# A feed-forward block's input differences: adding two pieces of a stored matrix in PSUM by products with the identity, instead of subtracting them one after the other

## The chip, the cores and the metric

The kernel runs on one core of a Trainium2 chip. The metric is the device time of one execution in microseconds (us), taken as the median of several. Five engines of the core work from lists of their own, each strictly in its list's order: TensorE (PE in the profile, with PEld for its weight loads) multiplies matrices into PSUM, VectorE (DVE), ScalarE (ACT) and GpSimd (POOL) work element by element, and SyncE (SP) issues the DMAs. They wait for one another through semaphores.

## The reference, cut to what matters

One layer: a norm, a combined projection, three kinds of mixing (Fourier, attention, gated delta rule), an output projection, and a squared-ReLU feed-forward block over 1024 positions with 1024 channels and 4096 hidden channels. The change lies in the last step, where the normed input `h` of the feed-forward block is prepared and multiplied by `w_ff1`.

```python
def _mlp(h, w1, w2):
    u = jnp.maximum(h @ w1, 0.0)
    return (u * u) @ w2

def _layer(x, xc, c, c_ctx, rope, lp, ctx_out):
    ...
    x = x + g1 * _mix_out(P, o_att, o_dn, lp['w_out'], lp['o_norm'])
    x = x + g2 * _mlp(_rms(x, lp['norm2']) * (1 + sc2) + sh2, lp['w_ff1'], lp['w_ff2'])
    ...
```

## The kernel before, in words

**Two pieces for one number.** Matrix products are done in a rounded float32 format in which one multiplication pass is enough. To keep accuracy every operand is cut in two: `hi` is the operand rounded (a copy, on ACT unless said otherwise), `lo` is the operand minus `hi`. `split` (L1452 to L1454) does this: L1453 is the rounding, L1454 the subtraction on the engine that it is given. A product is then three matmuls, hi by hi, hi by lo and lo by hi (`mm3`, L238 to L241).

**Seven products in place of eight.** The product `h @ w1` is cut into 2 by 2 blocks and done with seven block products instead of eight, which needs sums and differences of blocks on both sides. On the side of `h` the blocks are "11" and "21" (channels 0 to 511 and 512 to 1023 of the first 512 positions) and "12" and "22" (the same of the last 512 positions). Each is stored transposed, as four tiles k = 0 to 3 of 128 channels by 512 positions, with a hi and a lo piece each. `h2_first` (L1456) makes "11" and "21". `h2_second` (L1539) makes what the other products need: t1 = "12" - "11", t2 = "22" - t1, t3 = t2 - "11", t4 = t2 - "21", and "22" itself. A table (L1470) says which product takes which: s1 takes t1, s2 takes t2, s4 takes "22", s3 takes t3, and the product named 22 takes t4. The names 11 and 12 are the two products that need only what `h2_first` made.

**How h2_second works through its tiles.** `h2_T` (L1446) makes one tile: four transposes on PE (L244 in the profile, since the helper `tp` records them) into one PSUM bank, and one ACT instruction (L223, the helper `act`) that scales, shifts and moves the bank into SBUF. The banks come from the ring `tr2` of three, `bk0`, `bk1` and `bk3`. In a first loop over k, t1 is made from such a tile by two subtractions (L1540), first of the hi piece of "11", then of its lo piece, since only the pieces are kept. The first of the two is on POOL for k > 0 and on DVE for k = 0, the second on DVE. A second loop makes "22" and t2 (one subtraction). A third makes t3 and t4, each by two subtractions, the first on POOL, the second on DVE; the lo piece of t3 is also made on POOL.

**The products.** `ff1(j, name)` (L1564) does one of the seven products for 128 hidden channels, j counting them: 4 tiles by 3 matmuls of 128 by 512 into one bank of the ring `f1r`, which is A3[0], A3[1], A3[2], `bk2`, `bk3`, `bk4`. What follows in `ff1` takes the bank out: ACT for 11 and s1, DVE for the others (L1591 for 12, L1598 for s2, L1602 for s4, L1605 for s3, L1613 for 22), and makes the squares and sums that are stored to DRAM as `u`. So `bk3` serves both rings, and the s1 product of j = 0, which falls on `bk3`, can only come when `h2_second` is through with it. `w1_prep` (L1482) prepares the weight side: sums on POOL (L1487), hi pieces on ACT and lo pieces on DVE (`z1c` in the profile). `load_w1` (L1475) brings the weights (L1478 on SP's queue). `gate_bc` (L1347) makes rows of a gate with a short matmul into `bk0` and a DVE addition (L1352).

**What sets the order.** The kernel is written as one program; a scheduler at build time places the instructions of each engine in a fixed list by its own estimate of their times, with priorities given to pieces of the code. `h2_second` has such a priority (L1618), and so its instructions lie among those of the products 11 and 12 and of `w1_prep`. On the chip each engine keeps to its list. In the profile `fbase`, `rbase`, `z1c` and `z2b` are the large SBUF areas: `rbase` and `z2b` hold the pieces on the side of `h`, `z1c` those of the weights, `fbase` the full float32 tiles. `ba` and `bk` are the PSUM banks.

Of the kernel before, what the change touches and what calls it, by code (L numbers as in the profile page):

```python
# [14 lines left out]
ALU = mybir.AluOpType  # L15
AX = mybir.AxisListType

P = 128
# [176 lines left out]
def body(tc, t, out):  # L195
# [3 lines left out]
    with ctx:  # L199
# [14 lines left out]
        V, G, T, Y, SC = nc.vector, nc.gpsimd, nc.tensor, nc.sync, nc.scalar  # L214
# [4 lines left out]
        def rbuf(*shape, a=None):  # L219
            return Buf(a or Ra, (P,) + shape)  # L220
# [4 lines left out]
        def f32(ap):  # L225
            return ap.bitcast(F32)
# [8 lines left out]
        def mm(o, l, r, start, stop):  # L235
            pe(T.matmul(o, l, r, start=start, stop=stop))  # L236
# [15 lines left out]
        C = {k: cstb[a >= 256]()[:, a % 256 if a < 256 else a - 256 : b if a < 256 else b - 256] for k, (a, b) in CST.items()}  # L252
# [157 lines left out]
        for k, _ in enumerate(mod_steps(0, slabs, bk[2])):  # L410
            b = trb.next()
# [222 lines left out]
        b = gb.next()  # L634
# [795 lines left out]
        rw = [[buf(4, 256) for _ in range(2)], None]  # L1430
        shr = Ring([buf(512) for _ in range(3)])
        tr2 = Ring([bk[0], bk[1]])

        def rms_ff(q):
            st = rsb[q]()
# [16 lines left out]
        def split(i, hi, lo, eng, heng=None):  # L1452
            (heng or act)(hi, i)  # L1453
            eng.tensor_tensor(lo, i, f32(hi), op=ALU.subtract)  # L1454
# [82 lines left out]
        ur = Ring(slot[14:16] + slot[0:8:2] + slot[1:8:2] + slot[8:14])  # L1537

        def h2_second():  # L1539
            sub = lambda e, o, i, x: e.tensor_tensor(o, i, x, op=ALU.subtract)  # L1540
            t1, tr_ = [x() for x in slot[8:12]], Ring([x() for x in slot[12:14]])
            for k in range(4):
                h2_T(k, t1[k])
                sub(G if k > 0 else V, t1[k], t1[k], f32(HB["11"][k][0]))
                sub(V, t1[k], t1[k], f32(HB["11"][k][1]))
                split(t1[k], *HB["t1"][k], V)
            for k in range(4):
                h22 = tr_.next()
                h2_T(k + 4, h22)
                sub(V, t1[k], h22, t1[k])  # L1550
                split(t1[k], *HB["t2"][k], V)
                split(h22, *HB["22"][k], V)
            for k in range(4):
                x3 = tr_.next()
                sub(G, x3, t1[k], f32(HB["11"][k][0]))
                sub(V, x3, x3, f32(HB["11"][k][1]))
                split(x3, *HB["t3"][k], G)
                sub(G, t1[k], t1[k], f32(HB["21"][k][0]))
                sub(V, t1[k], t1[k], f32(HB["21"][k][1]))
                split(t1[k], *HB["t4"][k], V)  # L1560

        f1r = Ring(A3 + bk[2:5])
# [221 lines left out]
```

## Time and profile before

| | us |
|---|---|
| median of 3 runs (lowest, highest) | 1477.43 (1477.26, 1480.0) |
| the profiled execution: its own time | 1475.22 |
| its span on the core | 1473.1 |
| PE busy in the span | 1391.9 |
| DVE busy | 1026.7 |
| ACT busy | 704.6 |
| POOL busy | 657.2 |
| from 832.4 to 889.0, the stage of `h2_second`: length | 56.6 |
| in it: PE, DVE, ACT, POOL busy | 45.81, 53.34, 32.55, 43.45 |

The profiled execution lies 2.21 us under the median. The time outside the span is 1475.22 - 1473.1 = 2.1 us. Starts of instructions are counted in us from the start of the span. The column PEclk of a window is the TensorE clock that was granted in it, as a share of full speed.

### The profile page before, as it was taken

How to read it: one execution, taken by the hardware profiler on the slowest of the kernel's cores; microseconds unless marked ns; L12 is line 12 of the kernel's file. 1: busy time of each engine (PE TensorE's matmuls, PEld its weight loads, DVE VectorE, ACT ScalarE, POOL GpSimd, SP SyncE). 2: the span in 40 equal slices, each digit the busy share in tenths (PEclk: the TensorE clock that was granted, in tenths of full speed). 3: DMA queues.
4: the chain of work that ended last, by engine and by line, in shares of the span. 5: the costliest groups of instructions: out<-in, count | busy, mean ns of one | idle time of the engine just before them, and what ended most of it. 6: DMA issues, size and time to landing. Idle time of an engine off the chain costs nothing.

```text
span 1473.1 us, 28890 instructions
## 1 busy us (share of the span) xinstructions
PE 1391.9 (94%) x11438; PEld 1118.6 (76%) x11438; DVE 1026.7 (70%) x1747; ACT 704.6 (48%) x1239; POOL 657.2 (45%) x698
## 2 busy tenths in 40 slices
PE   5899888989999999989899789999999999999998
PEld 1787866766777777768799667888888888888886
DVE  0876688775878777786733898755556677676884
ACT  1743312223777777776512645554555443443331
POOL 2764653632446466465433866444343100020782
PEclk8799999989999999999999889999999999999999
DMA  9414374552001010042222214544445898776641
GB/s 327 176 58 141 95 186 122 148 109 79 9 9 25 5 36 10 10 148 72 87 82 105 92 49 143 164 152 156 158 157 185 296 395 271 249 236 210 200 158 57
DMA packets 137302, 197.65 MB, mean 134 GB/s; under 512 B 45021, under 2 KB 80463, under 8 KB 136911
## 3 DMA queue, kind: packets, MB, share of 16 engines
q1 hardware_dynamic: 136464, 195.12, 41.2%
q8 instruction: 89, 1.46, 0.4%
q10 hardware_dynamic: 703, 0.69, 0.2%
q14 instruction: 46, 0.38, 0.1%
HBM read 149.84 MB, written 45.94 MB: 133 GB/s over the span
## 4 chain that ended last, share of the span: by engine, by line
PE 46%; DVE 5%; POOL 2%; issue 1%; DMA 1%; ACT 0%; DVEq 0%; POOLq 0%; ACTq 0%; SPq 0%
PE bk L240 8%; PE bk L241 8%; PE bk L239 8%; PE ba L239 7%; PE ba L240 7%; PE ba L241 7%; DVE fbase L1540 1%; PE bk L236 1%; DVE z1c L1454 1%; DVE z1b L1321 0%; DVE rbase L984 0%; DMA fbase<-la 0%; POOL rbase L1454 0%; PE ba L236 0%; POOL z2c L1714 0%
## 5 line engine op out<-in xcount | busy, mean ns | idle before, releaser
L223 ACT ACTIVATE rbase<-fbase 128x512 fp32r<-128x512 f32 (+3 forms) x255 | 171.9, 686 | 87.6 <-PE bk L240 55.3
L223 ACT ACTIVATE fbase<-bk 128x512 f32<-128x512 f32 (+3 forms) x224 | 124.9, 561 | 150.8 <-PE bk L236 93.8
L236 PE MATMUL bk<-rbase 128*128 128x256 f32 (+1 forms) x960 | 164.5, 307 | 2.1 <-DVE rbase L984 1.1
L236 PEld LDWEIGHTS bk<-rbase 128*128 128x128 f32 (+1 forms) x960 | 127.0, 173 | 30.4 <-DVE rbase L984 1.9
L236 PE MATMUL ba<-rbase 128*65 128x512 f32 (+4 forms) x576 | 137.7, 341 | 6.3 <-DVE rbase L984 4.6
L223 ACT ACTIVATE z1c<-fbase 128x512 fp32r<-128x512 f32 (+1 forms) x120 | 76.7, 654 | 135.3 <-DMA fbase<-w_ff 49.1
L223 ACT ACTIVATE fbase<-fbase 128x512 f32<-128x512 f32 (+4 forms) x148 | 95.8, 660 | 94.5 <-POOL fbase L1606 27.2
L1487 POOL TENSOR_TENSOR fbase<-fbase 128x512 f32<-128x512 f32 x64 | 89.2, 1395 | 110.7 <-DVE z1c L1454 101.5
L1688 POOL TENSOR_TENSOR z2c<-z2c,fbase 128x512 f32<-128x512 f32 x16 | 31.8, 2010 | 203.6 <-ACT z2c L223 128.6
L960 DVE TENSOR_REDUCE fbase<-ba 128x1 f32<-128x512 f32 (+1 forms) x192 | 106.4, 594 | 19.6 <-PE ba L236 18.2
L223 ACT ACTIVATE rbase<-z1d 128x1024 fp32r<-128x1024 f32 x61 | 63.1, 1055 | 101.2 <-PE bk L240 87.3
L1454 DVE TENSOR_TENSOR z1c<-fbase,z1c 128x512 fp32r<-128x512 f32 x112 | 96.3, 866 | 19.2 <-ACT z1c L223 15.8
L1454 DVE TENSOR_TENSOR rbase<-z1d,rbase 128x1024 fp32r<-128x1024 f32 x61 | 85.5, 1416 | 31.8 <-ACT rbase L223 31.7
L984 POOL TENSOR_TENSOR rbase<-fbase,rbase 128x512 fp32r<-128x512 f32 x56 | 72.1, 1288 | 67.2 <-ACT rbase L223 63.1
L239 PE MATMUL bk<-rbase 128*128 128x512 f32 x256 | 99.6, 389 | 0.0
L240 PE MATMUL bk<-rbase 128*128 128x512 f32 x256 | 99.6, 389 | 0.0
L241 PE MATMUL bk<-rbase 128*128 128x512 f32 x256 | 99.6, 389 | 0.0
L984 DVE TENSOR_TENSOR rbase<-fbase,rbase 128x512 fp32r<-128x512 f32 x104 | 81.0, 779 | 24.6 <-ACT rbase L223 23.9
L1454 DVE TENSOR_TENSOR rbase<-fbase,rbase 128x1024 fp32r<-128x1024 f32 (+1 forms) x63 | 79.7, 1285 | 22.6 <-ACT rbase L223 22.5
L236 PEld LDWEIGHTS ba<-rbase 128*65 128x65 f32 (+1 forms) x576 | 75.7, 154 | 23.9 <-DVE rbase L984 5.7
L240 PE MATMUL ba<-rbase 128*128 128x512 f32 x192 | 74.7, 389 | 0.0
L241 PE MATMUL ba<-rbase 128*128 128x512 f32 x192 | 74.7, 389 | 0.0
(346 smaller groups left out, 3842.6 us busy)
## 6 DMA issues: line engine op xcount, KB each, us to landing
fbase<-w_ff SPq DMA_DIRECT2D x70, 512.0 KB
u<-fbase SPq DMA_DIRECT2D x112, 256.0 KB
z1d<-w_ff SPq DMA_DIRECT2D x34, 512.0 KB
z1d<-u SPq DMA_DIRECT2D x33, 512.0 KB
fbase<-w_mod SPq DMA_DIRECT2D x32, 512.0 KB
fbase<-u SPq DMA_DIRECT2D x23, 512.0 KB
z2a<-w_mod SPq DMA_DIRECT2D x16, 512.0 KB
fbase<-w_in SPq DMA_DIRECT2D x16, 512.0 KB
```

The source lines that it names most:

```text
L223: return SC.activation(o, i, f, **k)
L236: pe(T.matmul(o, l, r, start=start, stop=stop))
L239: pe(T.matmul(o, lh, rh, start=start, stop=False))
L240: pe(T.matmul(o, lh, rl, start=False, stop=False))
L241: pe(T.matmul(o, ll, rh, start=False, stop=stop))
L960: V.tensor_reduce(st4[:, z : z + 1], b, AX.X, ALU.max)
L984: (G if k2 in GP and not any(a <= n < b for a, b in NGP) else V).tensor_tensor(hl[:, :, 1], p, f32(hl[:, :, 0]), op=ALU.subtract)
L1454: eng.tensor_tensor(lo, i, f32(hi), op=ALU.subtract)
L1487: G.tensor_tensor(w[nm], w[a], w[b], op=op)
L1540: sub = lambda e, o, i, x: e.tensor_tensor(o, i, x, op=ALU.subtract)
L1688: G.tensor_tensor(c, c, G2[cs_.start // 512], op=ALU.mult)
```

## The change

The two subtractions of a stored block become one. PE adds hi and lo of a tile in a PSUM bank by two matmuls with an identity matrix as the stationary operand (`joined`), and DVE subtracts the bank from the tile. The bank comes from the ring `tr2`, in which the transposes also take theirs. This happens 12 times: four for t1, four for t3 and four for t4. No instruction of `h2_second` is on POOL any more; the lo piece of t3 is made on DVE. The identity is rounded once into the format of the products, into 128 columns of a buffer of its own.

```diff
@@ -1430,6 +1430,8 @@
         tr2 = Ring([bk[0], bk[1]])
+        idb = rbuf(P)
+        V.tensor_copy(idb(), C["ident"])
@@ -1537,26 +1539,30 @@
         def h2_second():
-            sub = lambda e, o, i, x: e.tensor_tensor(o, i, x, op=ALU.subtract)
+            sub = lambda o, i, x: V.tensor_tensor(o, i, x, op=ALU.subtract)
             t1, tr_ = [x() for x in slot[8:12]], Ring([x() for x in slot[12:14]])
+
+            def joined(nm, k):
+                b = tr2.next()
+                for z in range(2):
+                    mm(b, idb(), HB[nm][k][z], z == 0, z == 1)
+                return b
+
             for k in range(4):
                 h2_T(k, t1[k])
-                sub(G if k > 0 else V, t1[k], t1[k], f32(HB["11"][k][0]))
-                sub(V, t1[k], t1[k], f32(HB["11"][k][1]))
+                sub(t1[k], t1[k], joined("11", k))
                 split(t1[k], *HB["t1"][k], V)
             for k in range(4):
                 h22 = tr_.next()
                 h2_T(k + 4, h22)
-                sub(V, t1[k], h22, t1[k])
+                sub(t1[k], h22, t1[k])
                 split(t1[k], *HB["t2"][k], V)
                 split(h22, *HB["22"][k], V)
             for k in range(4):
                 x3 = tr_.next()
-                sub(G, x3, t1[k], f32(HB["11"][k][0]))
-                sub(V, x3, x3, f32(HB["11"][k][1]))
-                split(x3, *HB["t3"][k], G)
-                sub(G, t1[k], t1[k], f32(HB["21"][k][0]))
-                sub(V, t1[k], t1[k], f32(HB["21"][k][1]))
+                sub(x3, t1[k], joined("11", k))
+                split(x3, *HB["t3"][k], V)
+                sub(t1[k], t1[k], joined("21", k))
                 split(t1[k], *HB["t4"][k], V)
```

The scheduler places the lists anew between about 820 us and 930 us; ahead of that and behind it the lists of the compute engines hold the same instructions in the same order, with one more DVE copy for the identity. Lines behind the change have moved in the new file: the subtraction is L1542 (before L1540), the lo piece L1456 (L1454), and L1597, L1604, L1608, L1611, L1619 are the DVE evacuations of 12, s2, s4, s3 and 22. In the lists below `bk_76`, `bk_77`, `bk_78`, `bk_79` and `bk_80` are `bk0` to `bk4`, and `ba_73` to `ba_75` are A3[0] to A3[2].

TensorE, the first loop and the start of the second. First the list before: transposes for k = 3 to 7 (k = 0 to 2 were placed earlier), and the product s1 of j = 1 (`bk_80`, reading t1 from `z2b`).

```order
L244 MATMUL bk_79<-fbase 128x128 x4
L244 MATMUL bk_76<-fbase 128x128 x4
L244 MATMUL bk_77<-fbase 128x128 x4
L244 MATMUL bk_79<-fbase 128x128 x4
L239 MATMUL bk_80<-z2b,z1c 128x512
L244 MATMUL bk_76<-fbase 128x128 x4
L240 MATMUL bk_80<-z2b,z1c 128x512
```

The same place in the changed kernel:

```order
L236 MATMUL bk_79<-rbase 128x512 x2
L244 MATMUL bk_76<-fbase 128x128 x4
L236 MATMUL bk_77<-rbase 128x512 x2
L244 MATMUL bk_79<-fbase 128x128 x4
L239 MATMUL bk_80<-z2b,z1c 128x512
L240 MATMUL bk_80<-z2b,z1c 128x512
L241 MATMUL bk_80<-z2b,z1c 128x512
L236 MATMUL bk_76<-rbase 128x512 x2
L239 MATMUL bk_80<-z2b,z1c 128x512
L244 MATMUL bk_77<-fbase 128x128 x4
L240 MATMUL bk_80<-z2b,z1c 128x512
L241 MATMUL bk_80<-z2b,z1c 128x512
```

Joins (L236 of 128x512) stand between the groups of transposes in the same three banks, so that a group of transposes now follows a join out of a bank that DVE has to empty; the join for k = 0 stands a little ahead of this piece.

VectorE, from the end of the second loop into the third. The list before:

```order
L1540 TENSOR_TENSOR fbase<-fbase 128x512 x2
L1454 TENSOR_TENSOR rbase<-fbase,rbase 128x512 x4
L1540 TENSOR_TENSOR fbase<-fbase,rbase 128x512 x2
L1352 TENSOR_TENSOR fbase<-bk_76,fbase 128x256
L1454 TENSOR_TENSOR z1c<-fbase,z1c 128x512
L1540 TENSOR_TENSOR fbase<-fbase,rbase 128x512
L1454 TENSOR_TENSOR z1c<-fbase,z1c 128x512
L1540 TENSOR_TENSOR fbase<-fbase,rbase 128x512
```

And in the changed kernel:

```order
L1542 TENSOR_TENSOR fbase<-fbase 128x512 x2
L1456 TENSOR_TENSOR rbase<-fbase,rbase 128x512 x2
L1542 TENSOR_TENSOR fbase<-fbase,bk_79 128x512
L1456 TENSOR_TENSOR rbase<-fbase,rbase 128x512 x2
L1542 TENSOR_TENSOR fbase<-fbase,bk_76 128x512
L1542 TENSOR_TENSOR fbase<-fbase,bk_77 128x512
L1456 TENSOR_TENSOR rbase<-fbase,rbase 128x512
L1456 TENSOR_TENSOR z2b<-fbase,z2b 128x512
```

The subtractions of the third loop now read a PSUM bank and stand among the last lo pieces of the second loop, where before they came in a block behind it.

TensorE, the end of the third loop in the changed kernel:

```order
L236 MATMUL bk_76<-rbase 128x512 x2
L236 MATMUL bk_77<-rbase 128x512 x2
L240 MATMUL bk_80<-rbase,z1c 128x512
L236 MATMUL bk_79<-rbase 128x512 x2
L239 MATMUL ba_74<-z2b,z1c 128x512
L240 MATMUL ba_74<-z2b,z1c 128x512
L241 MATMUL ba_74<-z2b,z1c 128x512
L239 MATMUL ba_74<-z2b,z1c 128x512
L240 MATMUL ba_74<-z2b,z1c 128x512
L241 MATMUL ba_74<-z2b,z1c 128x512
L236 MATMUL bk_76<-rbase 128x512 x2
L239 MATMUL bk_79<-z2b,z1c 128x512
```

The last row is the start of the s1 product of j = 0 in `bk_79`. Before, that product came as soon as the last transposes had left the bank, in the middle of s2 and s4; now it follows the last joins, behind s2 and s4.

## The prediction

> **What bounds the kernel now.** I read the busy shares first, then the waits of PE, then windows around the stage of the change.
>
> ```profile
> span 1473.1 us, 28890 instructions
> PE 1391.9 (94%) x11438; PEld 1118.6 (76%) x11438; DVE 1026.7 (70%) x1747; ACT 704.6 (48%) x1239; POOL 657.2 (45%) x698
> ```
>
> PE is the bound over all, and the page alone would advise against giving it more work. The windows say where it is not. The first six columns are the window, its length, and the busy times of PE, PEld, DVE, ACT and POOL; then the granted clock.
>
> ```profile
> 834.30:849.00 14.70, 6.42 (x24) 3.99 (x23) 14.56 (x13) 10.75 (x19) 12.17 (x8) 0.60 0.30 90
> 849.00:855.00 6.00, 5.05 (x14) 3.48 (x13) 6.00 (x11) 5.31 (x10) 0.00 (x0) 0.57 0.12 45
> 855.00:870.00 15.00, 15.00 (x63) 11.21 (x62) 13.81 (x14) 5.77 (x10) 12.61 (x7) 1.00 0.02 3
> 870.00:880.00 10.00, 8.50 (x30) 5.31 (x29) 10.00 (x12) 4.11 (x7) 8.39 (x6) 0.90 0.33 101
> 880.00:885.00 5.00, 5.00 (x13) 3.39 (x11) 5.00 (x6) 2.12 (x5) 5.00 (x3) 0.51 0.02 3
> 893.20:1000.00 106.80, 106.05 (x459) 85.52 (x458) 76.24 (x107) 57.98 (x101) 50.12 (x36) 1.00 0.53 175
> 1000.00:1100.00 100.00, 100.00 (x434) 80.90 (x433) 56.30 (x86) 51.90 (x89) 42.84 (x31) 1.00 0.46 151
> ```
>
> From 834.3 to 885 DVE is busy without a break while PE idles or runs at half clock. Behind 893.2 PE has no idle time worth naming at full clock, so what PE gains before 893.2 reaches the end, and what it loses too. PE's longest wait in the stage, with total, count and longest, names who is late:
>
> ```profile
> PE bk L240 <- DVE z2b L1454: 5.8, 2, 4.9
> ```
>
> It is product s1 waiting for the lo pieces of t1. DVE's own work shows why, with POOL's beside it (count, busy, mean ns):
>
> ```profile
> L1540 DVE TENSOR_TENSOR fbase<-fbase,rbase 128x512 f32<-128x512 f32 x13 | 21.2, 1646 | 1.2 <-POOL fbase L1540 1.2
> L1454 DVE TENSOR_TENSOR z1c<-fbase,z1c 128x512 fp32r<-128x512 f32 x12 | 15.2, 1271 | 1.2 <-ACT z1c L223 1.2
> L1454 DVE TENSOR_TENSOR rbase<-fbase,rbase 128x512 fp32r<-128x512 f32 x8 | 5.1, 686 | 0.0
> L1591 DVE TENSOR_TENSOR fbase<-ba,fbase 128x512 f32<-128x512 f32 x1 | 0.7, 678 | 0.0
> L1540 POOL TENSOR_TENSOR fbase<-fbase,rbase 128x512 f32<-128x512 f32 x11 | 19.6, 1794 | 9.9 <-DVE rbase L1454 9.9
> L1454 POOL TENSOR_TENSOR z2b<-fbase,z2b 128x512 fp32r<-128x512 f32 x2 | 3.5, 1732 | 0.0
> L1454 POOL TENSOR_TENSOR rbase<-fbase,rbase 128x512 fp32r<-128x512 f32 x2 | 3.4, 1728 | 0.0
> ```
>
> The same kind of DVE instruction takes 686 ns or 1646: the long ones run beside POOL. L1591, which reads one operand from PSUM, takes 678, and not because POOL was quiet:
>
> ```profile
> 835.60 3.27 POOL L1487 TENSOR_TENSOR fbase<-fbase 128x512 f32<-128x512 f32 x2 [0.69 <-DVE z1c L1454]
> 835.98 0.68 DVE L1591 TENSOR_TENSOR fbase<-ba,fbase 128x512 f32<-128x512 f32 x1
> ```
>
> So a subtraction that reads a bank should keep its price beside POOL.
>
> **The unit prices.** From the timelines of PE and DVE:
>
> ```profile
> 816.61 0.60 PE L244 MATMUL bk<-fbase 128*128 128x128 f32 x4
> 816.97 0.37 PE L241 MATMUL ba<-z1c,rbase 128*128 128x256 f32 x1
> 848.45 0.80 PE L240 MATMUL bk<-z2b,z1c 128*128 128x512 f32 x1 [4.86 <-DVE z2b L1454]
> 851.05 0.80 PE L240 MATMUL bk<-z2b,z1c 128*128 128x512 f32 x1 [0.95 <-DVE z2b L1454]
> 854.66 0.39 PE L240 MATMUL ba<-rbase,z1c 128*128 128x512 f32 x1
> 854.89 0.40 PE L241 MATMUL ba<-rbase,z1c 128*128 128x512 f32 x1
> 879.49 0.79 PE L239 MATMUL ba<-rbase,z1c 128*128 128x512 f32 x1 [0.56 <-DVE fbase L1602]
> 883.50 0.63 PE L239 MATMUL ba<-rbase,z1c 128*128 128x512 f32 x1
> 883.93 0.63 PE L240 MATMUL ba<-rbase,z1c 128*128 128x512 f32 x1
> 884.91 0.69 PE L236 MATMUL bk<-fbase 1*128 1x256 f32 x2
> 885.53 0.74 PE L239 MATMUL ba<-z2b,z1c 128*128 128x512 f32 x2
> 893.22 0.39 PE L241 MATMUL bk<-rbase,z1c 128*128 128x512 f32 x1
> 849.11 0.69 DVE L1454 TENSOR_TENSOR z1c<-fbase,z1c 128x512 fp32r<-128x512 f32 x1
> 849.71 0.68 DVE L1540 TENSOR_TENSOR fbase<-fbase,rbase 128x512 f32<-128x512 f32 x1
> ```
>
> By their starts: a 128x512 matmul 0.233 us at full clock (854.66 to 854.89) and 0.43 at half; a group of four transposes 0.36; a gate row 0.62; a DVE instruction that is not held up 0.60. A join has the form of a product's matmul, so two cost 0.47.
>
> **The change part by part.** Removed: 13 DVE subtractions (21.2 us) and all of POOL's 11 (19.6), with POOL's four lo pieces of t3 (3.5 + 3.4). Added on DVE: 12 subtractions that read PSUM and 4 lo pieces, 16 at 0.60 = 9.6. Added on PE: 24 matmuls, 24 x 0.233 = 5.6 at full clock, 24 x 0.43 = 10.3 at half. The copy of the identity, one DVE instruction long before, is nothing: PE is the bound there. DVE's list from the first lo piece at 833.6 to the end of `h2_second` has 51 instructions now, 51 x 0.60 = 30.6, so it could be through by 864.2, where it now needs until
>
> ```profile
> 887.99 1.01 DVE L1454 TENSOR_TENSOR z1c<-fbase,z2b 128x512 fp32r<-128x512 f32 x1 [0.70 <-ACT z2b L223]
> ```
>
> It will not be, since it waits: for POOL's weight sums at first, for ACT's hi pieces in the second loop, for PE in the third. So I make the sum on PE, from 834.3, where its first long stall begins, to the last matmul of product 12 of j = 2, which starts at 893.22 and is the first point that both lists reach with the same products done.
>
> *Before:* 58.9 us elapsed for 144 matmuls x 0.233 = 33.6, five groups of transposes 1.8, four gate rows 2.5: 37.9 of work, 21.0 lost.
>
> *After:* 144 products and 22 joins (two come earlier), 166 x 0.233 = 38.7; six groups of transposes 2.2; three gate rows 1.9: 42.8 of work. Its losses, by walking the new lists with the prices above:
>
> - 834.3 to 849.5, the first loop. Nothing moves until ACT takes the first transposes out of their bank:
>
> ```profile
> 835.47 0.76 ACT L223 ACTIVATE fbase<-bk,fbase 128x512 f32<-128x512 f32 x1
> 833.63 2.43 DVE L1454 TENSOR_TENSOR z1c<-fbase,z1c 128x512 fp32r<-128x512 f32 x2 [1.23 <-ACT z1c L223]
> 837.66 3.43 DVE L1540 TENSOR_TENSOR fbase<-fbase,rbase 128x512 f32<-128x512 f32 x2
> ```
>
>  Then join 1 can go (836.3), and join and transposes alternate through three banks, each waiting for DVE or ACT, at half clock and without long gaps. DVE comes to the first subtraction at 837.7 as before, since the same weight pieces stand ahead of it (from 833.63), and is through with it at 838.3 in place of 841.1 (837.66 + 3.43, both pieces). The hi piece follows on ACT behind three others (0.5 to 0.7 each) by 839.6, the lo piece on DVE behind a second subtraction and one weight piece beside POOL by about 841, where the list before has it at 848.4 (the end of the 4.86 us wait); the last at 848.4. PE gets through six transpose groups, 8 joins and 14 products: 2.2 + 22 x 0.233 = 7.3 of 15.2 us. Lost 7.9.
> - 849.5 to 863.5: 48 products of s2 and s4 and 12 joins, 14.0, as the pieces come: two pairs are ready when it starts, the other two at about 855. Lost 0.
> - 863.5 to 870.6: product 22 of j = 1 needs the bank of s2, which DVE empties at 864.7 behind two lo pieces of weights; s1 of j = 0 needs the bank of the last t3 join (866.5). 22 products and a gate row take 5.7. Lost 1.4.
> - Behind that the last pieces, 0.4, and 1.3 as an estimate for the 0.1 us between engines at some dozen hand-overs that the walk passes over.
>
> Sum 7.9 + 1.4 + 0.4 + 1.3 = 11.0 lost, 53.8 elapsed: 888.1. One gate row that was in the sum before comes later now, 0.6. Gain 893.2 - 0.6 - 888.1 = 4.5 us. In the profiled execution 1475.2 becomes 1470.7; that lies 2.2 under the median, so **1477.4 - 4.5 = 1472.9, say 1473**. From both sides: with no loss at all the gain would be 893.2 - 0.6 - 834.3 - 42.8 = 15.5; with the old losses it would be 4.9 below nothing.
>
> What is late next: ACT, whose list holds weight pieces that wait for a DMA ahead of hi pieces of t3 and t4. The loads are issued when the old weights have been split:
>
> ```profile
> 868.59 3.87 SPq L1478 DMA_DIRECT2D fbase<-w_ff x2
> ACT z1c L223 <- DMA fbase<-w_ff: 3.4, 2, 2.5
> ```
>
> I let this cost nothing, because the hi pieces behind it are wanted only near 870; uncovered it is the 3.4 us of this row.
>
> **The clock, and a rule against the change.** At 851.05 PE starts a dense run at half clock, and at 854.66 it is at full: 3.6 us. The run from 879.49 needs some 6. Both are products without transposes between them. I let the joins, transposes and products from 838 on do the same by about 845. If only an unmixed run lifts the clock, it rises 3.6 us after 849.5, and half of the work of these 3.6 us is lost, 1.8: a gain of 2.7, 1474.7. That is a rival below. The Trainium skill, "TensorE: Matmul & The Clock Gate", Part 4 (PE-mode transpose), is the rule that speaks for it: transposes are not counted as activity. Its section on a second failure mode adds that cycling through PSUM banks can make the clock swing.
>
> **The rivals.** *DVE keeps its pace (slower).* Every join of the third loop waits for a bank that DVE empties, and the s1 product of j = 0, which helped to fill PE between 855 and 870, now stands behind them. So PE is tied to DVE's list. Behind DVE's last piece PE still has, by the new list, 62 matmuls and two gate rows, 15.7. If the 51 instructions take with their waits the mean of this stage,
>
> ```profile
> 832.40:889.00 56.60, 45.81 (x163) 31.95 (x164) 53.34 (x55) 32.55 (x55) 43.45 (x26) 0.79 0.15 47
> ```
>
> 53.34 / 55 = 0.97 us, the list ends at 883.1, and PE at 898.8 instead of 892.6: 6.2 slower, 1484. It decides from 0.85 us an instruction upward (892.6 - 15.7 - 833.6 = 43.3 over 51); my walk has 0.73. For it: POOL still has four weight sums from 835.60 on, and weight pieces beside such sums took 1271 ns in the mean. Against it: at 3.27 for two they end near 842, and 12 of 16 subtractions read PSUM.
>
> *ACT paces it (no change).* Fewer waits for DVE, but the same ACT work, 32.55 in the stage, now in a shorter one, in list order behind sums and DMAs. If the 3.4 us above is paid in full, 1.1 of the gain is left: 1476.
>
> *Late clock (no change).* As above: 1474.7, under 3 us of gain.
>
> *PE finds everything ready.* If the first loop loses half of what I gave it and nothing else is lost but 1.3, losses are 5.2 and the gain 10.3: 1467.
>
> *Half clock until the joins are through.* 60 matmuls from 849.5 at 0.43 instead of 0.233 are 11.8 more, less the 1.4 of waits they would cover: 10.4 less gain, 1483. The two runs above speak against it, since joins and products together are dense.
>
> That the change does not do what it says I leave out: the new lists have the joins and none of the POOL work.
>
> **How the numbers follow.** Chances: my forecast (gain 2 to 8 us) 0.47, everything ready 0.12, ACT 0.13, late clock 0.08, DVE's pace 0.15, half clock 0.05. A measurement of this kernel tells about 0.2%, 3 us, from no change. The forecast case gives 0.43 to faster and 0.04 to the same; with the 0.12 faster is 0.55; the same is 0.04 + 0.13 + 0.08 = 0.25; slower 0.20. The range takes in the ready case at 1467 and reaches toward the two slower ones, to 1481, which leaves out a part of each end; the forecast's own range is 1469.5 to 1475.5.
>
> **What would show it.** Right: joins of 0.233 us at full clock; subtractions from PSUM at about 0.68 whatever POOL does; the last of DVE's `h2_second` near 871; the first lo piece of t1 near 841; PE's 4.9 us wait gone; full clock from about 845 and no second drop near 880. Wrong if DVE's list ends later than about 877, if PE waits again for more than 4 us in one place behind 849.5, or if the time of the stage moves and the end does not.

## The result

The changed kernel takes 1470.1 us (median of 4 runs, 1468.1 to 1471.1) where the kernel before took 1478.4 beside it (4 runs, 1477.3 to 1480.0): a ratio of 0.9941, with a 95% interval of 0.9924 to 0.9959. That is a gain of 8.7 us by the ratio, 6.1 to 11.2; the difference of the medians is 8.3. The prediction was a gain of 4.5 and 1473. The profiled execution took 1469.3 (before: 1475.2).

Of the page of the changed kernel, the span and the busy times:

```profile
span 1467.5 us, 28926 instructions
...
PE 1391.6 (95%) x11462; PEld 1119.5 (76%) x11462; DVE 1011.8 (69%) x1751; ACT 703.0 (48%) x1239; POOL 631.3 (43%) x683
```

PE has 24 matmuls more and is busy for 0.3 us less than before (1391.9): a matmul of 128 by 512 at half clock takes 0.43 us from start to start instead of 0.233, and fewer run at half clock. Spans of two executions can't be subtracted yet, though, for the stage doesn't come at the same time in each of them. The last normalisation ahead of it, from the timelines of DVE, in the kernel before, in the changed one, and in a second profile of the changed one:

```profile
830.62 1.78 DVE L1444 TENSOR_SCALAR fbase<-fbase 128x1024 f32<-128x1024 f32 x1 [0.44 <-POOL fbase L1440]
```
```profile
832.65 1.77 DVE L1446 TENSOR_SCALAR fbase<-fbase 128x1024 f32<-128x1024 f32 x1 [0.45 <-POOL fbase L1442]
```
```profile
831.00 1.77 DVE L1446 TENSOR_SCALAR fbase<-fbase 128x1024 f32<-128x1024 f32 x1 [0.44 <-POOL fbase L1442]
```

One and the same kernel has it at 832.65 and at 831.00. So I read the stage from this instruction on: from it to the end of the span it is 1473.1 - 830.62 = 642.5 us before, and 634.9 and 635.0 in the two profiles of the changed kernel, **7.6 us less**. This "rest" is given for every run below; what happened ahead of that instruction does not enter it.

Windows of equal length, each shifted with that instruction (window, length, busy times of PE, PEld, DVE, ACT, POOL, granted clock, DMA share, GB/s), before:

```profile
834.32:849.62 15.30, 7.02 (x26) 4.32 (x24) 15.16 (x14) 11.37 (x20) 12.15 (x8) 0.59 0.29 87
849.62:870.62 21.00, 20.05 (x77) 14.86 (x76) 19.81 (x24) 10.79 (x19) 12.61 (x7) 0.89 0.07 19
870.62:886.62 16.00, 14.50 (x46) 9.30 (x45) 16.00 (x17) 7.03 (x12) 15.02 (x9) 0.79 0.18 59
```

And in the changed kernel:

```profile
836.35:851.65 15.30, 11.05 (x49) 8.02 (x49) 15.25 (x21) 14.05 (x25) 7.18 (x5) 0.89 0.32 104
851.65:872.65 21.00, 20.43 (x87) 15.64 (x86) 19.03 (x32) 12.67 (x23) 1.62 (x1) 1.00 0.08 26
872.65:888.65 16.00, 16.00 (x67) 12.05 (x66) 12.92 (x16) 6.90 (x13) 12.12 (x8) 1.00 0.37 118
```

In the first 15.3 us PE gets through 49 matmuls (each transpose counts as one) where it had 26. Its clock is 1.00 in both windows behind that, and from 872.65 to 888.65 it doesn't idle. DVE is as full as before in the first window, with 21 instructions instead of 14: it is not less busy there, it does more.

DVE's rows that answer to those of the prediction, from the groups by form and the timeline of the changed kernel:

```profile
L1542 DVE TENSOR_TENSOR fbase<-fbase,bk 128x512 f32<-128x512 f32 x12 | 7.8, 678 | 1.3 <-PE bk L236 1.3
```
```profile
839.68 1.27 DVE L1542 TENSOR_TENSOR fbase<-fbase,bk 128x512 f32<-128x512 f32 x2
...
841.60 1.65 DVE L1456 TENSOR_TENSOR z2b<-fbase,z2b 128x512 fp32r<-128x512 f32 x1
...
865.17 0.68 DVE L1604 TENSOR_TENSOR fbase<-ba,fbase 128x512 f32<-128x512 f32 x1
...
871.81 0.69 DVE L1456 TENSOR_TENSOR z1c<-fbase,z2b 128x512 fp32r<-128x512 f32 x1
```

The subtractions that read a bank cost 678 ns in the mean (1646 before, from SBUF). Two of them together take 1.27 us while POOL is in the middle of four weight sums:

```profile
837.61 6.78 POOL L1489 TENSOR_TENSOR fbase<-fbase 128x512 f32<-128x512 f32 x4 [0.70 <-DVE z1c L1456]
```

The Trainium skill, "SBUF — State Buffer", in "Who interferes with whom", has the rule for that: a DVE instruction with two SBUF inputs contends with a GpSimd instruction that reads SBUF, one with at most one SBUF input, outside the modes that use both of DVE's ports, doesn't. The rows here agree.

What PE still waits for in the stage (total, count, longest):

```profile
PE bk L244 <- DVE fbase L1542: 2.5, 3, 1.4
PE bk L236 <- ACT fbase L223: 1.8, 1, 1.8
PE bk L244 <- DVE fbase L1446: 0.9, 1, 0.9
PE ba L239 <- DVE fbase L1604: 0.6, 1, 0.6
```

The wait of 4.9 us for the lo pieces of t1 is gone. In the first row transposes wait for banks that DVE has to empty, as the new order makes them do. Only the last of the four rows lies behind the first loop.

### The profile page after: what moved, and what is told of

The parts are those of the page before. It is cut to its first block, busy times and chain, and to the rows that moved or that the text cites. A ratio compares the mean times of both kernels' runs of the same rounds, so it can differ in the third digit from the quotient of the medians.

```text
span 1467.5 us, 28926 instructions
## 1 busy us (share of the span) xinstructions
PE 1391.6 (95%) x11462; PEld 1119.5 (76%) x11462; DVE 1011.8 (69%) x1751; ACT 703.0 (48%) x1239; POOL 631.3 (43%) x683
## 4 chain that ended last, share of the span: by engine, by line
PE 49%; DVE 2%; POOL 1%; issue 1%; ACT 1%; DVEq 0%; POOLq 0%; ACTq 0%
PE bk L240 8%; PE bk L241 8%; PE bk L239 8%; PE ba L239 8%; PE ba L241 8%; PE ba L240 8%; PE bk L236 2%; PE ba L236 1%; DVE z1b L1321 0%; POOL rbase L1456 0%; DVE z1c L1456 0%; DVE rbase L984 0%; ACT z1c L223 0%; POOL z2c L1720 0%; POOL z2b L1284 0%
## 5 line engine op out<-in xcount | busy, mean ns | idle before, releaser
L236 PE MATMUL bk<-rbase 128*128 128x256 f32 (+2 forms) x984 | 173.1, 311 | 4.6 <-ACT fbase L223 2.5
L236 PEld LDWEIGHTS bk<-rbase 128*128 128x128 f32 (+1 forms) x984 | 132.6, 175 | 34.2 <-ACT fbase L223 3.7
L236 PE MATMUL ba<-rbase 128*65 128x512 f32 (+4 forms) x576 | 139.8, 345 | 5.1 <-DVE rbase L984 3.6
L1456 DVE TENSOR_TENSOR z1c<-fbase,z1c 128x512 fp32r<-128x512 f32 x112 | 91.3, 820 | 24.6 <-ACT z1c L223 21.1
L1456 DVE TENSOR_TENSOR rbase<-z1d,rbase 128x1024 fp32r<-128x1024 f32 x61 | 85.0, 1410 | 26.6 <-ACT rbase L223 26.4
L1456 DVE TENSOR_TENSOR rbase<-fbase,rbase 128x1024 fp32r<-128x1024 f32 (+1 forms) x65 | 81.4, 1270 | 20.9 <-ACT rbase L223 20.6
L236 PEld LDWEIGHTS ba<-rbase 128*65 128x65 f32 (+1 forms) x576 | 77.0, 156 | 23.3 <-DVE rbase L984 4.8
```

## The experiments

In this section a join is the pair of matmuls that fills one bank: four joins (eight matmuls) for t1, eight (sixteen matmuls) for t3 and t4. A kernel with joins for t1 alone makes the other subtractions in two steps, and the other way round.

Theory: PE's time was lost because DVE came too late to the lo pieces of t1 in the first loop, and then too late to the pieces of the third; subtracting a joined bank halves the number of DVE's and POOL's subtractions of stored pieces, and such a subtraction is not slowed by POOL. The rival: what helps is that POOL no longer stands in DVE's way, and the joins are no more than the means to take it off. Each kernel ran five rounds beside the kernel before. "Rest" is from the last normalisation to the end of the span in its profile.

| kernel | us | ratio to before | 95% interval | rest, us |
|---|---|---|---|---|
| before | 1477.8 to 1478.6 | 1 | | 642.5 |
| the identity's copy alone | 1478.2 | 1.0001 | 0.9989 to 1.0012 | 643.4 |
| joins for t1, the rest as before | 1472.3 | 0.9967 | 0.9950 to 0.9983 | 638.4 |
| joins for t3 and t4, t1 as before | 1474.5 | 0.9981 | 0.9971 to 0.9991 | 641.1 |
| no joins, all on DVE | 1475.4 | 0.9991 | 0.9979 to 1.0003 | 640.4 |
| joins for t3 and t4, t1 on DVE | 1477.4 | 0.9993 | 0.9981 to 1.0004 | 641.8 |
| joins for t1, the rest on DVE | 1470.7 | 0.9952 | 0.9936 to 0.9967 | 637.3 |
| the change again | 1470.0 | 0.9944 | 0.9928 to 0.9960 | 635.0 |
| the change, t3's lo pieces on POOL | 1469.3 | 0.9939 | 0.9926 to 0.9951 | 634.9 |
| the change, all joins twice | 1472.1 | 0.9959 | 0.9946 to 0.9973 | 637.5 |
| the change, t1's joins twice | 1468.8 | 0.9930 | 0.9916 to 0.9944 | 634.7 |
| the change, transposes one ahead | 1469.6 | 0.9936 | 0.9919 to 0.9953 | 635.8 |
| the change, transposes four ahead | 1472.5 | 0.9958 | 0.9942 to 0.9975 | 636.3 |

The rests rank the kernels nearly as the timed ratios do. Each comes from one profile: the two kernels that have the stage as before differ by 0.9 us (642.5 and 643.4), the two profiles of the change by 0.2. So where I speak of a difference of 1 or 2 us, both have to show it.

### The anchor and the control

The change again, without an edit:

> The changed kernel once more, unchanged, as the anchor for the runs beside it. If the gain of 8.3 us (ratio 0.994) is the change's own, it is 0.993 to 0.996 again, and the profile again has the stage of the change coming about 2 us later than in the kernel before (the last carry-free weight sum ahead of it, line 1446, at about 832.6 where the kernel before has 830.6). If those 2 us are chance of one execution, they are gone here.

The ratio came again, and the 2 us of later arrival did not (831.00). The control is the kernel before with

```diff
+        idb = rbuf(P)
+        V.tensor_copy(idb(), C["ident"])
```

> The kernel before with the copy of the identity alone: one buffer and one DVE instruction more, nothing else. If the 2 us by which the stage comes later in the changed kernel are due to this copy or its buffer, it is 1 to 2 us slower than the kernel before (1.0007 to 1.0014), and the last weight sum ahead of the stage is at 832.6. Otherwise it is the same (0.999 to 1.001), at 830.6.

It is the same as the kernel before. Its one profile has the normalisation (L1446, which the two expectations call a weight sum) at 832.71, which alone would have looked like the copy's doing; the time says that it costs under 1.8 us (1.0012) and most likely nothing, as the prediction had it.

### One part alone

Joins for t1 only (the edit is shown against the kernel before):

```diff
-                sub(G if k > 0 else V, t1[k], t1[k], f32(HB["11"][k][0]))
-                sub(V, t1[k], t1[k], f32(HB["11"][k][1]))
+                sub(t1[k], t1[k], joined("11", k))
...
                 sub2(G, x3, t1[k], f32(HB["11"][k][0]))
                 sub2(V, x3, x3, f32(HB["11"][k][1]))
```

> Joins for t1 alone (the first loop, 8 matmuls); t3 and t4 subtract in two steps on POOL and DVE as in the kernel before, and POOL makes t3's lo pieces. Theory one (what counts is that the first loop's subtractions come from PSUM, so that the first lo piece is there at 841 and not 848): most of the gain is here, PE's 4.9 us wait for the lo pieces of t1 is gone and the ratio is 0.995 to 0.997 (4 to 7 us faster). Theory two (DVE's whole list sets the pace, and POOL beside it in the third loop makes it slow): DVE still ends its last h2_second near 885, PE waits there instead, and under 3 us of gain are left (0.998 to 1.000).

Joins for t3 and t4 only (against the kernel before):

```diff
                 sub2(G if k > 0 else V, t1[k], t1[k], f32(HB["11"][k][0]))
                 sub2(V, t1[k], t1[k], f32(HB["11"][k][1]))
...
-                sub(G, x3, t1[k], f32(HB["11"][k][0]))
-                sub(V, x3, x3, f32(HB["11"][k][1]))
-                split(x3, *HB["t3"][k], G)
-                sub(G, t1[k], t1[k], f32(HB["21"][k][0]))
-                sub(V, t1[k], t1[k], f32(HB["21"][k][1]))
+                sub(x3, t1[k], joined("11", k))
+                split(x3, *HB["t3"][k], V)
+                sub(t1[k], t1[k], joined("21", k))
```

> Joins for t3 and t4 alone (the third loop, 16 matmuls, t3's lo pieces on DVE); t1 subtracts in two steps on POOL and DVE as in the kernel before. Theory one: the 4.9 us wait of PE for the lo pieces of t1 stays, the gain is only the idle and half-clock time around 870 to 885, 1 to 3 us (0.998 to 0.9995). Theory two: DVE's last h2_second is early by 8 us or more and most of the gain is here (0.995 to 0.997). If the two parts add up, this ratio's gain and that of the joins for t1 alone give 8.3 us together.

By the ratios 4.9 us (2.5 to 7.4) and 2.8 (1.3 to 4.3); together 7.7, so the parts add up within their intervals. Theory one is the better one for size: the four joins of t1 bring more than the eight others. The kernel with joins for t3 and t4 alone is the telling one. Its first loop is as late as before, and PE waits as before; DVE, however, is through early (PE's and DVE's timelines):

```profile
854.05 0.80 PE L240 MATMUL bk<-z2b,z1c 128*128 128x512 f32 x1 [4.87 <-DVE z2b L1456]
```
```profile
836.22 1.77 DVE L1446 TENSOR_SCALAR fbase<-fbase 128x1024 f32<-128x1024 f32 x1 [0.44 <-POOL fbase L1442]
...
880.12 0.68 DVE L1456 TENSOR_TENSOR z1c<-fbase,z2b 128x512 fp32r<-128x512 f32 x1
```

So DVE's last piece of `h2_second` comes 43.9 us behind the normalisation, where before it came 57.4 behind (887.99 - 830.62). DVE is through 13.5 us earlier, and the rest is shorter by 1.4 to 2.3 us only. So theory two's main claim falls: that DVE's list ends early is not what most of the gain is made of. What its words said of the joins for t1 alone was partly seen: DVE's last piece is at 887.60 in that kernel, 56.1 behind the normalisation, and PE has a new wait, 4.38 us for a gate row's bank:

```profile
869.69 1.22 PE L236 MATMUL bk<-fbase 1*128 1x256 f32 x2 [4.38 <-DVE fbase L1352]
```

because DVE comes to the row that empties this bank only behind two-step subtractions that POOL slows (its timeline, and its group of these subtractions):

```profile
865.88 3.42 DVE L1543 TENSOR_TENSOR fbase<-fbase,rbase 128x512 f32<-128x512 f32 x2
869.23 0.41 DVE L1352 TENSOR_TENSOR fbase<-bk,fbase 128x256 f32<-128x256 f32 x1
```
```profile
L1543 DVE TENSOR_TENSOR fbase<-fbase,rbase 128x512 f32<-128x512 f32 x8 | 12.1, 1540 | 0.0
```

### POOL taken away without joins

All subtractions in two steps on DVE, t3's lo pieces on DVE (against the kernel before; the first steps for t3 and t4 move from POOL to DVE in the same way):

```diff
-                sub(G if k > 0 else V, t1[k], t1[k], f32(HB["11"][k][0]))
-                sub(V, t1[k], t1[k], f32(HB["11"][k][1]))
+                sub2(V, t1[k], t1[k], f32(HB["11"][k][0]))
+                sub2(V, t1[k], t1[k], f32(HB["11"][k][1]))
...
-                split(x3, *HB["t3"][k], G)
+                split(x3, *HB["t3"][k], V)
```

> No joins at all: all subtractions in two steps on DVE, t3's lo pieces on DVE too, and nothing of it on POOL. PE has 24 matmuls (5.6 us) less than in the changed kernel, DVE 12 instructions more. Theory one (the joins are what is worth the time, since each halves the number of DVE's subtractions): DVE's list has 63 instructions; at the 0.725 us each that it took in the changed kernel that is 45.7 us, so it ends 8.7 us later than in the changed kernel, and the time is that of the kernel before or up to 3 us above (1.000 to 1.002). The rival (it is only that POOL is off DVE's back, the 1646 ns instructions): two-step subtractions at 0.60 to 0.69, about as fast as the changed kernel, 0.993 to 0.996, and better if the joins' PE time counts.

The gain is 1.3 us (-0.4 to 3.1), of the change's 8.3: outside both expectations, much nearer to theory one's. PE still waits 4.0 us for the first lo piece of t1 (4.9 before), and DVE's last piece of `h2_second` comes 15.5 us later than in the change, where 8.7 were expected. The rival falls as an account of the whole, though its mechanism is real: the 24 two-step subtractions now cost

```profile
L1543 DVE TENSOR_TENSOR fbase<-fbase,rbase 128x512 f32<-128x512 f32 x24 | 19.0, 820 | 0.0
```

820 ns in place of 1646, yet DVE has 24 of them in place of 13. To see it in the first loop alone, t1 in two steps on DVE, t3 and t4 with joins, so that POOL has no subtraction of `h2_second` anywhere (against the changed kernel):

```diff
-                sub(t1[k], t1[k], joined("11", k))
+                sub2(V, t1[k], t1[k], f32(HB["11"][k][0]))
+                sub2(V, t1[k], t1[k], f32(HB["11"][k][1]))
```

> Joins for t3 and t4; t1 subtracts in two steps, all on DVE, so that POOL has no subtraction anywhere. It closes the square with three runs so far: joins everywhere 1470.0, joins for t3 and t4 with t1 on POOL and DVE 1474.5, no joins and all on DVE 1475.4. If POOL beside DVE is what makes the first loop late, this is close to the changed kernel, 1470 to 1471.5 (0.994 to 0.9955). If what counts in the first loop is that a subtraction is one instruction and reads PSUM (four DVE instructions fewer there, and those from PSUM cost 0.60 to 0.68 beside POOL's weight sums), it is 1473 to 1475 (0.9965 to 0.998), and PE still waits over 3 us for a lo piece of t1.

It was slower than either expectation: a gain of 1.0 us, -0.6 to 2.8. That is 7.2 us behind the changed kernel, which differs from it in the four joins of t1 alone. DVE's timeline and PE's there:

```profile
837.55 1.77 DVE L1446 TENSOR_SCALAR fbase<-fbase 128x1024 f32<-128x1024 f32 x1 [0.44 <-POOL fbase L1442]
...
844.59 5.24 DVE L1543 TENSOR_TENSOR fbase<-fbase,rbase 128x512 f32<-128x512 f32 x5
...
853.47 0.68 DVE L1456 TENSOR_TENSOR z2b<-fbase,z2b 128x512 fp32r<-128x512 f32 x1
```
```profile
854.20 0.79 PE L240 MATMUL bk<-z2b,z1c 128*128 128x512 f32 x1 [2.97 <-DVE z2b L1456]
```

Five two-step subtractions stand ahead of the first lo piece of t1, and they cost 1.05 us each beside POOL's weight sums, which remain. The piece comes 15.9 us behind the normalisation (853.47 - 837.55), against 17.1 before (847.72 - 830.62), by the row

```profile
847.72 0.68 DVE L1454 TENSOR_TENSOR z2b<-fbase,z2b 128x512 fp32r<-128x512 f32 x1
```

and 8.95 in the changed kernel (841.60 - 832.65). Taking POOL's subtractions off moves it by 1.2 us, the joins by 7.0 more. These 7.0 have two parts that no run here separates: a subtraction from a bank is shorter beside POOL's weight sums (0.64 us against 1.05), and the list that the scheduler made with joins has two subtractions ahead of this piece where the list without them has seven.

### Do the joins of the third loop earn their PE time?

Joins for t1, the others in two steps on DVE (against the changed kernel):

```diff
-                sub(x3, t1[k], joined("11", k))
-                split(x3, *HB["t3"][k], V)
-                sub(t1[k], t1[k], joined("21", k))
+                sub2(V, x3, t1[k], f32(HB["11"][k][0]))
+                sub2(V, x3, x3, f32(HB["11"][k][1]))
+                split(x3, *HB["t3"][k], V)
+                sub2(V, t1[k], t1[k], f32(HB["21"][k][0]))
+                sub2(V, t1[k], t1[k], f32(HB["21"][k][1]))
```

> Joins for t1 alone; t3 and t4 subtract in two steps on DVE, none of it on POOL. Against the changed kernel PE saves 16 matmuls (16 x 0.233 = 3.7 us), DVE has 8 instructions more (8 x 0.60 = 4.8 us or 8 x 0.725 = 5.8). If PE's own work sets the time of the third loop (PE was busy from 850 to 865 without a gap), it is up to 3.7 us faster than the changed kernel (0.991 to 0.994). If DVE's list sets it, it is up to 5 us slower than the changed kernel (0.995 to 0.998).

The second branch: 0.9952, and a rest 2.3 us longer than the change's; the timed intervals overlap, so that these joins earn something is likely, not shown by the time. Its windows, of the same lengths and places as those above:

```profile
838.40:853.70 15.30, 10.64 (x49) 7.95 (x49) 15.26 (x21) 14.04 (x25) 7.20 (x5) 0.89 0.33 104
853.70:874.70 21.00, 19.57 (x77) 14.28 (x76) 20.30 (x29) 9.50 (x17) 6.42 (x5) 0.95 0.10 27
874.70:890.70 16.00, 14.72 (x52) 10.88 (x52) 12.42 (x20) 7.37 (x13) 1.41 (x1) 0.85 0.12 34
```

The first window is the changed kernel's. Behind it PE idles 1.4 and 1.3 us and its clock falls again: 16 matmuls (3.7 us) are saved, and more than that is lost in waits and at half clock. Still, this kernel without the joins of the third loop has 7.1 us of the gain (4.9 to 9.5).

Four of the kernels have no subtraction of `h2_second` on POOL and make a square. The joins of t1 bring 7.2 us in it where t3 and t4 have joins (0.9993 to 0.9944) and 5.8 where they have none (0.9991 to 0.9952). The joins of t3 and t4 bring 1.2 us beside those of t1 (0.9952 to 0.9944), and nothing without them (0.9991 and 0.9993; the rest is 1.4 us longer). And the joins for t1 alone bring 4.9 us with the third loop's first steps on POOL and 7.1 with all of it on DVE, where a two-step subtraction takes 884 ns instead of 1540; the rest is 1.1 us shorter, and the intervals overlap. So the 2.8 us of the joins for t3 and t4 alone may be in part POOL's absence from the third loop, which that kernel has too; no run settles the shares.

Doubling prices a join in its place. All of them twice, as the edit shows, then those of t1 alone:

```diff
-                for z in range(2):
-                    mm(b, idb(), HB[nm][k][z], z == 0, z == 1)
+                for z in range(4):
+                    mm(b, idb(), HB[nm][k][z % 2], z % 2 == 0, z % 2 == 1)
```

> The changed kernel with each of the 12 joins made twice in its bank (24 matmuls more, the second pair overwrites the first), which prices a join in its place. If PE has no room anywhere behind 834, it is 24 x 0.233 = 5.6 us slower than the changed kernel (ratio about 0.998). If, as the walk of the prediction has it, the first loop has PE time to spare and the third has none, the joins of t1 (8) cost nothing and those of t3 and t4 (16) 3.7 us: 1473 to 1474 (0.996 to 0.997). If PE waits for DVE in the third loop too, next to nothing: 0.994 to 0.995.

> The changed kernel with the four joins of t1 made twice (8 matmuls more), those of t3 and t4 once. All twelve made twice cost about 2 us. If the first loop has PE time to spare, these 8 cost 0 to 0.5 us (0.994 to 0.995) and the 2 us are the third loop's. If PE's place in the order makes each of them late for DVE, 1 to 2 us (0.995 to 0.996).

All twice: the rest is 2.6 us longer than the change's, the time 2.1. Those of t1 twice: 634.7, nothing (the time, 1468.8, is not above the change's either). So eight more matmuls in the first loop are free, as the first branch of the second expectation had it, and sixteen more in the third cost 2.1 to 2.6 of their 3.7 us. PE is full there with all joins doubled:

```profile
850.99:871.99 21.00, 21.00 (x91) 16.67 (x90) 17.67 (x29) 11.85 (x22) 1.60 (x1) 1.00 0.10 30
871.99:887.99 16.00, 16.00 (x67) 11.61 (x66) 13.01 (x15) 8.01 (x14) 11.15 (x7) 1.00 0.21 70
```

And the four lo pieces that moved to DVE, moved back (`split(x3, *HB["t3"][k], G)`):

> The changed kernel with the four lo pieces of t3 back on POOL, as in the kernel before. They took 1.73 us each there against 0.60 to 0.69 on DVE, and in the changed kernel POOL is idle for 21 us in that stage. Theory (DVE's list is tight, moving them to it cost 4 x 0.6 = 2.4 us): 1 to 2 us faster than the changed kernel. Rival (a lo piece on POOL is 1.1 us later and makes DVE's instructions beside it slow): same or up to 3 us slower, 0.994 to 0.996.

No difference (634.9 against 634.9 and 635.0), as the rival's lower end had it. DVE's last piece comes 0.6 us earlier (870.97, that is 38.6 behind the normalisation, against 39.2), and the end doesn't move: DVE's list is not what the third loop of the changed kernel waits for.

### Looking for more in the first loop

In the changed kernel most of what is still lost lies in the first loop. Two orders tried to shorten the transposes' waits:

```diff
-            for k in range(4):
-                h2_T(k, t1[k])
+            h2_T(0, t1[0])
+            for k in range(4):
+                if k < 3:
+                    h2_T(k + 1, t1[k + 1])
                 sub(t1[k], t1[k], joined("11", k))
                 split(t1[k], *HB["t1"][k], V)
```

> The changed kernel, with the transposes of the next column block issued ahead of each join of the first loop. In the changed kernel's profile the first loop still loses 7.6 us of PE time, in waits of transposes for banks that a DVE subtraction has to empty (2.5 us in three). If these waits set the pace, it is 1 to 2 us faster than the changed kernel (0.993). If the lo pieces that DVE makes in its own order set it, it is the same or up to 1 us slower, since the first lo piece of t1 moves behind another subtraction.

> The same with all four transposes of the first loop ahead of its four joins. If the transposes' waits for a bank set the pace, 1 to 3 us faster than the changed kernel (0.992 to 0.9935); if the first join, which now comes three transposes later, delays DVE's subtractions and the lo pieces of t1, 1 to 3 us slower (0.995 to 0.997).

One ahead is not told apart from the change (0.9936; a rest 0.8 to 0.9 us longer), four ahead has a rest 1.3 to 1.4 longer and a time 2.4 us above; neither is faster, and the first lo piece comes at 12.0 and 12.3 us behind the normalisation instead of 8.95. So this piece can come 3 us later for some 1 us, since PE has transposes and joins to do meanwhile; with four ahead, the longest wait of PE in the stage is one of 1.77 us behind the second loop, for the bank that s1 of j = 0 takes over from a join. No version beat the change by more than the intervals leave open.

## Why the prediction was right, and short

**What bounds the kernel: right.** PE's losses ahead of 893 reached the end. The last matmul of product 12 of j = 2 and what waited behind it, in the changed kernel and, for the second, in the kernel before:

```profile
887.77 0.40 PE L241 MATMUL bk<-rbase,z1c 128*128 128x512 f32 x1
```
```profile
911.09 0.47 PE L239 MATMUL ba<-z2b,z1c 128*128 128x512 f32 x1 [0.75 <-DVE fbase L1598]
```

From that matmul to the end it was 1473.1 - 893.22 = 579.9 us before and 1467.5 - 887.77 = 579.7 now: the gate row that moved behind it adds 0.6, and the 0.75 us wait of the second row, which is of the kernel before, is gone.

**The sum.** The forecast's gain was 2 to 8 us and its time 1469.5 to 1475.5. The time lies in it (1470.1), near its lower end; the gain is past it (8.3 by the medians), because the kernel before took 1478.4 beside the change and not 1477.4. So the direction and the place of the gain were foreseen, and its size was short by nearly half. Shifted by the later arrival (2.03), the stretch that began at 834.3 begins at 836.33; 887.77 - 836.33 = 51.4 us elapsed, where the prediction had 53.8 with the same 42.8 of work. Lost: 8.6 instead of 11.0. Term by term:

- The first loop, 7.9: measured 7.6. From 836.33 to 849.62, 13.3 us, PE has six groups of transposes, six matmuls of joins and nine of products, 2.2 + 15 x 0.233 = 5.7. The prediction's stretch goes on for another 1.9 us, to 851.53, in which PE has no idle.
- Behind it, 1.4 + 0.4 + 1.3 = 3.1: measured 1.0. **This is the term that was mis-sized.** Of the two waits in the 1.4, the one for s2's bank took 0.57:

```profile
866.00 0.47 PE L239 MATMUL ba<-z2b,z1c 128*128 128x512 f32 x1 [0.57 <-DVE fbase L1604]
```

 and s1 of j = 0, which the walk let wait for the bank of the last t3 join, follows the join ahead of it without an idle (PE's timeline):

```profile
867.46 0.62 PE L236 MATMUL bk<-rbase 128*128 128x512 f32 x2
867.93 0.39 PE L239 MATMUL bk<-z2b,z1c 128*128 128x512 f32 x1
```

 The allowance of 1.3 for hand-overs found nothing to stand for: from 851.65 to 872.65 PE is busy for 20.43 of 21.00 us, and the 0.57 left are that one wait. The other 0.4 of the 1.0 lies in no wait that the profile shows.
- The 0.75 us wait at 911 was no term of the sum.

So the gain in the profile, from the arrival on, is 4.5 + (11.0 - 8.6) + 0.75 = 7.65, what the rests show. Two slips of the prediction do not enter the sum: with the old losses the gain would be 5.5 below nothing (15.5 - 21.0), not 4.9; and DVE was not busy without a break from 834.3 to 885, for it idles 1.19 us before 860.02, in a window in which PE itself was busy throughout at full clock.

**Which part brings it: half right.** That the first loop's subtractions come early and PE's 4.9 us wait goes was the step that carries: the joins of t1 alone bring 4.9 us, and 7.1 with POOL off the third loop. The mark that I set for DVE, the last piece of `h2_second` near 871, was met (871.81, with a later arrival of 2) but is no measure of the gain, as the kernel with joins for t3 and t4 alone shows.

**Prices: right.** 678 ns for a subtraction from PSUM whatever POOL does; of the joins' 24 matmuls, the eight in the first loop are free and the sixteen others are paid for in part, going by what a second set of them cost. I had put the joins' cost in the sum as work in both loops, which does no harm, since what was lost in the first loop, 7.9, is what is left of its length beside that work.

**ACT and its DMA waits at nothing: right.** ACT still waits for weights (0.69 us at 868.40), and PE has no wait for ACT behind the first loop.

**The clock, and the rival that spoke against the change.** The clock did rise in the run of joins, transposes and products, and did not fall again in the changed kernel. Windows around the drop in its two profiles, and the whole loop with t1's joins made twice:

```profile
840.65:844.65 4.00, 4.00 (x15) 3.10 (x14) 3.95 (x4) 4.00 (x8) 3.66 (x3) 0.57 0.33 93
844.65:849.65 5.00, 3.87 (x24) 2.74 (x24) 5.00 (x9) 4.80 (x9) 0.00 (x0) 1.00 0.58 191
```
```profile
837.80:844.30 6.50, 5.53 (x18) 4.30 (x19) 6.46 (x8) 6.39 (x12) 4.87 (x3) 0.50 0.38 123
844.30:848.00 3.70, 3.17 (x22) 2.64 (x21) 3.70 (x7) 3.30 (x7) 0.00 (x0) 0.96 0.45 142
```
```profile
833.45:850.45 17.00, 13.58 (x66) 9.49 (x66) 15.78 (x21) 15.17 (x27) 8.72 (x6) 1.00 0.28 88
```

Half clock for some 3, some 6.5, and 0 us, and the rests are 634.9, 635.0 and 634.7: inside this loop the clock is worth nothing, since PE waits for DVE anyway.

Behind the loop it is worth something, and a part of the gain is there. In the kernel before, the half clock outlasted PE's long wait: the prediction's row from 849.00 to 855.00 has 14 matmuls in 6.00 us at a clock of 0.57. The changed kernel has, a little earlier in the stage,

```profile
850.00:855.00 5.00, 5.00 (x24) 3.98 (x23) 4.60 (x9) 5.00 (x10) 0.00 (x0) 1.00 0.14 52
```

As an estimate, some 12 matmuls at 0.43 instead of 0.233 are 2.4 us, and the 12 of the second run at half clock, from 879.49 on, another 2.4. The three kernels without joins for t1 (joins for t3 and t4 with t1 as before, no joins, t1 on DVE) have a clock of 0.52, 0.50 and 0.50 in the 6.2 us that begin 17.8 us behind the normalisation, as the kernel before has with 0.54; the change and the two kernels with joins for t1 alone have 1.00. So in these runs early pieces of t1 and a full clock in this stretch always came together. No run fills PE in the first loop without bringing the pieces early, so the shares of the two in the 5 to 7 us of t1's joins stay open; by the estimate the clock's is at most some 2.4.

The late-clock rival needed half clock until some 3.6 us into the dense run behind the first loop; it was full by 844.7 in both profiles, ahead of that run. The Trainium skill, "TensorE: Matmul & The Clock Gate", Part 1, says that the activity window runs free, so that the same kernel meets it at another phase each time; the two profiles of one kernel agree with that. Its rule that transposes don't count (Part 4) did not keep the clock down here; as a rule for transposes alone it isn't tested by these rows, for joins and products stood between them.

**The rivals.** DVE's pace would have needed 0.85 us an instruction; from 835.65 to 872.50 (871.81 + 0.69) its 51 took 36.9 us, 0.72. Everything ready asked for 5.2 us of losses and there were 8.6; the time landed between it and the forecast. Half clock until the joins are through was seen nowhere.

## What to carry to other kernels

When an engine is late, look for the first result that the bound engine waits for and count what stands ahead of it in the late engine's list; making the whole list shorter is worth little until that first result moves (13.5 us off the end of DVE's list bought 1.4 to 2.8 us, 8 us off its first lo piece some 5). That result's date is a guide and not the measure: once the bound engine has other work meanwhile, 3 us of it cost only some 1. Work for the bounding engine is free in the stretch where it waits and costs most of its price in the stretch where it doesn't: double it there, in place, to find out which of the two it is. Look also at the clock behind a wait: here the matmuls that came after it were slow for another 6 us. And before two profiles are subtracted, line them up at the last instruction ahead of the change.

## What the runs showed that I had not expected

The two halves of the change may help each other: by the rests, joins for t1 bring 6 to 7 us when t3 and t4 have joins, and 4 to 5 when these are made the old way (641.1 or 641.8 to 634.9; 642.5 or 643.4 to 638.4). By the timed ratios the halves add up (4.9 + 2.8 against 8.3), so this is not settled. And the same stretch of one kernel ran at half clock for 3 us in one execution and for 6.5 in another. With t1's joins made twice it did not drop at all. But the kernel with all joins twice has the same eight matmuls more in this loop, and there the clock was 0.50 from 839.99 to 842.99, so these matmuls alone do not keep it up.
